# Up projection of a gated FFN by seven block products instead of eight, and its down-projection sums kept in DRAM

## The chip, the cores and the metric

One Trainium2 chip, one of its cores. The metric is the device time of one execution of the whole program in microseconds. The kernel before takes 2612.33 us (median of three runs, 2606.83 to 2616.81).

## The reference

One layer of a diffusion backbone on 512 tokens of 2048 features, all in float32. First a token mixer (a gated MLP with a spatial product), whose result is added to the stream. Then the part that the change touches:

```python
n_l = modulate(rmsnorm(h_lat, norm_g[i, 1]), m_l[:, :, 3], m_l[:, :, 4])
h_lat = h_lat + m_l[:, :, 5] * conv_ffn(n_l, ffn_w_up[i], ffn_conv_w[i], ffn_conv_b[i], ffn_w_down[i])
return rmsnorm(h_lat, final_g)

def conv_ffn(h, w_up, conv_w, conv_b, w_down):
    z = dwconv(h @ w_up, conv_w, conv_b, FFN_CONV // 2)   # width 3, over the tokens
    g, v = jnp.split(z, 2, axis=-1)
    return (jax.nn.silu(g) * v) @ w_down
```

`w_up` is 2048 x 11264 (a gate part `g` and a value part `v` of 5632 columns each), `w_down` is 5632 x 2048.

## The kernel before

Every tile has 128 partitions. Features lie on the partitions and the 512 tokens along the free axis, so a matmul takes a 128 x 128 block of weights as the stationary operand and a 128 x 512 tile of tokens as the moving one. A float32 operand is split into two float32r parts, high and low (`split`, lines 69 to 71: ScalarE copies the high part, VectorE subtracts it), and a product is three matmuls: high by high, high by low, low by high (`mm3`, line 64). Weights come in loads of 512 KB into a pool of six buffers, `r`; the split parts, `wh` and `wl`, have three buffers each. One such load with its matmuls is a *unit*. The weights of a unit are loaded and split two units ahead (`LOOK = 2`, line 878); with three buffers a split waits until TensorE has left the buffer of three units before.

The program is a list of units worked off by the loop at line 860. Other work (making normalised tiles, moving sums out of PSUM) is put in a list, `deferred`, and taken from it by `pop` at fixed places between the units. From this the framework's scheduler makes one instruction list for each engine; each engine works its own list off in order.

The FFN runs in eleven chunks of 512 columns of the gate part and the same columns of the value part. The normalised tokens are sixteen tiles `n2h`, `n2l`.

- **First chunk, gate part** (`f0_comp`, line 676): sixteen units, eight for each half of the tokens, since the norm's factors (`n_spread`) of the first half are known before those of the second. These matmuls have 256 columns, three times eight to a unit. Beside them `n_tile` (line 617) makes the normalised tiles.
- **First chunk, value part, and every later chunk** (`f_comp`, line 662): eight units for the gate part and eight for the value part, 24 matmuls of 512 columns each, into four PSUM banks.
- **Evacuation** (`conv_evac`, line 640): the width-3 convolution over the tokens, by ScalarE and VectorE straight out of PSUM; SiLU, the product with the gate, and a split into the operands of the down projection (`gated`).
- **Down projection** of the chunk before (`d_comp`, line 717): eight units, 24 matmuls of 512 columns each; VectorE adds each finished bank to the residual tile `ht[d]` in SBUF (`d_evac`, line 701).
- **Last chunk's down projection** (`e_comp`, line 787): in two halves of the tokens, with the final norm.

From the second chunk on the order is 16 units up, 8 units down.

Of the kernel before, what the change touches and what calls it, by code (L numbers as in the profile page):

```python
# [7 lines left out]
F32 = mybir.dt.float32  # L8
# [15 lines left out]
# the v half of w_in, as (column group, first K tile, end): short pieces while  # L24
# the modulation is still coming in
# [11 lines left out]
def build(tc, ctx, x, xT, cvec, adaT, ada_b, norm_g, w_in, g_v, w_sT, b_s, w_out,  # L37
# [6 lines left out]
    wpool = ctx.enter_context(tc.tile_pool(name="wpool", bufs=3))  # L44
# [14 lines left out]
    def mm(out, lhsT, rhs, first, last):  # L59
        nc.tensor.matmul(out, lhsT, rhs, start=first, stop=last)  # L60
# [3 lines left out]
    def mm3(out, sh, sl, mh, ml, first, last):  # L64
        mm(out, sh, mh, first, False)
        mm(out, sh, ml, False, False)
        mm(out, sl, mh, False, last)
# [22 lines left out]
    def load_cb():  # L90
        """silu(c) along every partition, by products that pick one row of [4, 512]."""
# [49 lines left out]
    def rstd_cols(ss, n, w, out=None):  # L141
        """1 / sqrt(ss / n + eps) of [P, w] sums: the table's root, then one Newton step."""
# [12 lines left out]
    def sum_cols(tiles, w):  # L155
        """Per-token sums over the feature partitions of the tiles: [P tokens, w] in PSUM."""
# [7 lines left out]
    def spread(r, w):  # L164
        """[P tokens, w] to [P, w * P], all tokens along every partition."""
# [138 lines left out]
    # the other tiles, in steps that are spread over the products  # L304
# [32 lines left out]

    deferred = []
# [6 lines left out]
    units = []          # (prep, comp, after)  # L345

# [100 lines left out]
    def sp_comp(cg, c4):  # L447
        # one moving operand holds both parts of the spatial weights side by side
# [60 lines left out]
    def sq_acc(key, d, ts=slice(0, T)):  # L509
        """Adds the square of a tile's tokens; the very last one is kept apart."""  # L510
# [51 lines left out]
    # the last K tiles of the second pass go in two halves of the tokens, so that  # L562
    # the norm of the first half runs under the products of the second
# [17 lines left out]
    def oh_comp(th, i):  # L581
        def f(w):
# [26 lines left out]
    n2h, n2l = [None] * ND, [None] * ND  # L609

    nstat, n2r = {}, {}
    made = [0, 0]

# [313 lines left out]
```

## Time and profile before

| | |
|---|---|
| median of three runs | 2612.33 us (2606.83 to 2616.81) |
| profiled execution, from its first instruction to its last | 2610.5 us |
| TensorE busy in it | 2560.6 us, 98% |
| VectorE busy | 1408.2 us, 54% |
| ScalarE busy | 855.5 us, 33% |
| GpSimd busy | 0.7 us |
| DMA, mean over the span | 138 GB/s |

What the device spends around the first and last instruction is not shown apart; the span lies 1.8 us under the median of the runs and inside their spread. Three stretches matter. The first chunk's gate part runs from 1149.6 to 1197.5 us, its value part to 1241.0, and then ten chunks of 130.6 us each follow, up to 2546.6. The rest, to 2610.5, is the last down projection with the final norm.

The engines' names in the rows are PE (TensorE matmul), PEld (TensorE weight load), DVE (VectorE), ACT (ScalarE), POOL (GpSimd) and SP (SyncE, which issues DMAs). In a row "wl<-r,wh" is the tile written and the tiles read; "b" is any tile of the general pool of 70, "p" a PSUM bank.

### The profile page before, as it was taken

The page shows a single profiled execution, that of the slowest core. Times are in us where ns is not written, and L with a number is a line of the kernel's source. Part 1 is how long each engine was busy: PE and PEld are TensorE (multiplying, and loading weights), DVE is VectorE, ACT ScalarE, POOL GpSimd, SP SyncE. Part 2 cuts the span into 40 slices and gives each one's busy share as a digit, 9 for nine tenths or more (in the row PEclk, how much of TensorE's full clock was granted, in tenths as well). Part 3 has the DMA queues.
Part 4 walks back from the last instruction along what each step waited for, and adds up shares of the span by engine and source line. Part 5 has one row for each costly group of instructions (what it writes and reads, how often), then busy time and mean ns, then how long its engine had stood idle before and what let it go on. Part 6 is the DMA issues. An engine that isn't in the chain of part 4 may idle for free.

```text
span 2610.5 us, 29733 instructions
## 1 busy us (share of the span) xinstructions
PE 2560.6 (98%) x11816; PEld 2135.1 (82%) x11816; DVE 1408.2 (54%) x2179; ACT 855.5 (33%) x1211; POOL 0.7 (0%) x6
## 2 busy tenths in 40 slices
PE   6999999999999999999999999999999999999998
PEld 5888788788888888898888888888888888888888
DVE  6885578666566446465453535353535353535365
ACT  7422234333334224355322222222222222222234
POOL 0000000000000000000000000000000000000000
PEclk9999999999999999999999999999999999999998
DMA  7886555555555446524233333333333333323331
GB/s 265 293 284 198 173 173 179 174 171 177 177 168 193 154 145 194 185 82 133 96 97 97 98 96 97 96 98 96 97 97 97 96 98 97 97 97 97 96 104 65
DMA packets 157556, 360.84 MB, mean 138 GB/s; under 512 B 12132, under 2 KB 18404, under 8 KB 157416
## 3 DMA queue, kind: packets, MB, share of 16 engines
q1 hardware_dynamic: 155304, 356.84, 42.1%
q10 hardware_dynamic: 2112, 2.10, 0.2%
q8 instruction: 92, 1.51, 0.2%
q14 instruction: 48, 0.39, 0.0%
HBM read 354.70 MB, written 4.19 MB: 137 GB/s over the span
## 4 chain that ended last, share of the span: by engine, by line
PE 76%; DMA 12%; DVE 8%; issue 3%; ACT 1%; SPq 0%; DVEq 0%; ACTq 0%
PE p L60 76%; DMA r<-in_adaT 10%; DVE wl L71 3%; DVE r L129 2%; DMA r<-in_w_in 1%; DVE b L361 1%; ACT wh L70 0%; DVE b L462 0%; DVE sp L444 0%; DVE b L465 0%; DVE b L71 0%; DVE r L781 0%; ACT b L268 0%; DVE b L356 0%; ACT b L70 0%
## 5 line engine op out<-in xcount | busy, mean ns | idle before, releaser
L60 PE MATMUL p<-b,wh 128*128 128x512 f32 (+1 forms) x6208 | 1883.5, 386 | 0.0
L60 PEld LDWEIGHTS p<-b,wh 128*128 128x128 f32 x6208 | 1158.0, 188 | 230.8
L60 PE MATMUL p<-b,wl 128*128 128x512 f32 (+1 forms) x3104 | 1196.0, 385 | 0.0
L71 DVE TENSOR_TENSOR wl<-r,wh 128x1024 fp32r<-128x1024 f32 (+1 forms) x457 | 550.9, 1206 | 795.7 <-ACT wh L70 793.5
L70 ACT ACTIVATE wh<-r 128x1024 fp32r<-128x1024 f32 (+1 forms) x457 | 478.2, 1047 | 1503.9 <-PE p L60 1474.9
L60 PEld LDWEIGHTS p<-b,wl 128*128 128x128 f32 x3104 | 584.5, 188 | 116.8
L129 DVE SCALAR_TENSOR_TENSOR r<-r,cb 128x1024 f32<-128x1024 f32 x192 | 233.6, 1223 | 295.5 <-DMA r<-in_adaT 295.1
L60 PE MATMUL p<-wh,b 128*128 128x512 f32 x992 | 314.1, 395 | 1.7 <-ACT wh L70 1.7
L60 PEld LDWEIGHTS p<-wh,b 128*128 128x128 f32 x992 | 188.4, 190 | 41.6 <-ACT wh L70 2.7
L60 PE MATMUL p<-wl,b 128*128 128x512 f32 x496 | 195.9, 395 | 8.8 <-DVE wl L71 8.8
L701 DVE SCALAR_TENSOR_TENSOR b<-p,m,b 128x512 f32<-128x512 f32 x160 | 118.0, 748 | 42.7 <-PE p L60 42.6
L60 PEld LDWEIGHTS p<-wl,b 128*128 128x128 f32 x496 | 94.4, 190 | 31.4 <-DVE wl L71 11.9
L60 PE MATMUL p<-b 128*128 128x256 f32 (+1 forms) x624 | 84.5, 296 | 5.3 <-ACT b L70 5.3
L60 PEld LDWEIGHTS p<-b 128*128 128x128 f32 x624 | 79.1, 193 | 9.0 <-ACT b L70 6.7
L70 ACT ACTIVATE b<-t 128x512 fp32r<-128x512 f32 (+1 forms) x91 | 48.8, 549 | 38.1 <-DVE t L654 37.5
L71 DVE TENSOR_TENSOR b<-t,b 128x512 fp32r<-128x512 f32 (+1 forms) x91 | 53.0, 592 | 10.6 <-ACT b L70 9.4
L60 PE MATMUL p<-sp 128*128 128x256 f32 x256 | 40.5, 294 | 9.2 <-DVE sp L444 8.3
L361 DVE TENSOR_TENSOR b<-p,b 128x512 f32<-128x512 f32 x76 | 48.9, 682 | 0.0
L60 PEld LDWEIGHTS p<-sp 128*128 128x128 f32 x256 | 36.2, 192 | 15.1 <-DVE sp L444 12.0
L71 DVE TENSOR_TENSOR b<-b 128x512 fp32r<-128x512 f32 (+2 forms) x69 | 43.3, 660 | 4.1 <-ACT b L70 4.0
L443 ACT ACTIVATE sp<-b,rv 128x128 fp32r<-128x128 f32 x128 | 42.1, 388 | 7.4 <-DVE sp L444 4.6
L645 ACT ACTIVATE t<-p,cw 128x512 f32<-128x512 f32 x44 | 34.2, 776 | 23.4 <-PE p L60 12.2
(86 smaller groups left out, 777.0 us busy)
## 6 DMA issues: line engine op xcount, KB each, us to landing
r<-in_adaT SPq DMA_DIRECT2D x192, 512.0 KB, 4.5
r<-in_w_up SPq DMA_DIRECT2D x184, 512.0 KB, 3.5
r<-in_w_in SPq DMA_DIRECT2D x121, 512.0 KB, 4.4
r<-in_w_down SPq DMA_DIRECT2D x88, 512.0 KB, 3.6
r<-in_w_out SPq DMA_DIRECT2D x64, 512.0 KB, 4.6
b<-in_x SPq DMA_DIRECT2D x16, 256.0 KB, 5.4
b<-in_xT SPq DMA_DIRECT2D x16, 256.0 KB, 5.2
r<-in_w_in SPq DMA_DIRECT2D x14, 256.0 KB, 4.1
```

The costliest lines, as they stand in the source:

```text
L60: nc.tensor.matmul(out, lhsT, rhs, start=first, stop=last)
L70: nc.scalar.activation(hi, src, AF.Copy)
L71: nc.vector.tensor_sub(lo, src, hi.bitcast(F32))
L129: nc.vector.scalar_tensor_tensor(r[b], r[b], 1.0, state["cb"][b], op0=ALU.mult, op1=ALU.mult, accum_out=m2[:, b, j:j + 1])
L361: nc.vector.tensor_add(b, p, b)
L443: nc.scalar.activation(vh[:, ns], v, AF.Copy, scale=rv[:, n:n + 1])
L645: nc.scalar.activation(t, p, AF.Identity, bias=cw[:, 3, ct:ct + 1], scale=cw[:, 1, ct:ct + 1])
L701: nc.vector.scalar_tensor_tensor(ht[d], p, m[:, 5 * ND + d:5 * ND + d + 1], ht[d], op0=ALU.mult, op1=ALU.add)
```

## The change

1. **Seven block products.** In the chunks after the first, the up projection treats two K tiles, two blocks of 128 weight columns and the two halves of the tokens as a 2 x 2 by 2 x 2 product of blocks and forms it by Strassen's method in Winograd's form: seven products in place of eight. A unit holds two pairs of K tiles, so 2 x 7 x 3 = 42 matmuls of 256 columns; a group of four units (`up_group`) gives two output tiles. `s_prep` forms four sums of weight blocks on VectorE (lines 778 to 780) before it splits seven blocks of 128 columns for each K pair; `s_evac` recombines the seven sums from four banks into the two output tiles, in SBUF (`z`), and `conv_evac` reads `z`.
2. **Sums of the tokens.** `n_tile` normalises in place and `t_pair` forms the sums of token blocks once, as new float32r tiles `x1` to `x4`. The first chunk keeps the eight plain products, by halves of the tokens (`f_mm`); its value part (`f1_comp`) goes by halves too, so it has 384 matmuls of 256 columns in place of 192 of 512.
3. **Residual in DRAM.** The new tiles take the room of `ht`. The residual is written to a DRAM tile `hD` at the end of the mixer (32 DMAs on SP's queue, in `oh_comp`). `d_evac` is now a ScalarE copy out of PSUM with the gate as scale, into a pool `part` of three buffers, and a DMA from GpSimd's queue that adds the tile to `hD`: 16 in each of ten chunks. Beside the last of them the sixteen tiles are read back.
4. **Order.** From the second chunk on: one group of four units, four units down, one group, four units down, two groups; in the last such round two, two and then four units down, these with the loads of the last chunk's weights.
5. **Small things.** The pool of split weights has four buffers, not three. `w_up` is laid out by blocks in DRAM. The signs of odd output tiles are put into the convolution's weights (two small VectorE instructions in `late_consts`). The pop after a unit comes behind the next load from the FFN on.

```diff
-    wpool = ctx.enter_context(tc.tile_pool(name="wpool", bufs=3))
+    wpool = ctx.enter_context(tc.tile_pool(name="wpool", bufs=4))
+    part = ctx.enter_context(tc.tile_pool(name="part", bufs=3))
+    dram = ctx.enter_context(tc.tile_pool(name="dram", bufs=1, space=bass.MemoryType.DRAM))
...
             sq_acc("2", 8 + i, ts)
+            for d in (i, 8 + i):
+                nc.sync.dma_start(out=hD[d * P:(d + 1) * P, ts], in_=ht[d][:, ts])
...
+    def t_pair(p):
+        def f():
+            e, o = ht[2 * p], ht[2 * p + 1]
+            t = tmp_t()
+            nc.vector.tensor_sub(t[:, L], o[:, R], e[:, R])
+            nc.vector.tensor_sub(e[:, R], e[:, L], e[:, R])
+            nc.vector.scalar_tensor_tensor(o[:, R], e[:, R], -1.0, o[:, R], op0=ALU.mult, op1=ALU.subtract)
+            nc.vector.scalar_tensor_tensor(t[:, R], o[:, R], -1.0, o[:, L], op0=ALU.mult, op1=ALU.subtract)
+            h, l = pair_t(x2, p)
+            split(h[:, R], l[:, R], e[:, R])
+            split(*pair_t(x3, p), t)
+            x4[p] = blk_t(F32R)
+            split(x4[p][:, L], x4[p][:, R], o[:, R])
+            tmade[0] += 1
         return f
...
+        if th == 1:
+            for p in range(NP):
+                deferred.append(t_pair(p))
...
+    def s_prep(cp, u):
+        def f():
+            r = wload(w_up[cp, u].rearrange("p k b -> p k b"), 2, 512).rearrange(
+                "p (k b c) -> p k b c", k=2, b=4)
+            s = raw.tile([P, 1024], F32, tag="r", name="s").rearrange("p (k b c) -> p k b c", k=2, b=4)
+            nc.vector.tensor_add(s[:, :, 0:2, :], r[:, :, 0:1, :].to_broadcast([P, 2, 2, P]), r[:, :, 1:4:2, :])
+            nc.vector.tensor_add(s[:, :, 2, :], s[:, :, 1, :], r[:, :, 1, :])
+            nc.vector.tensor_add(s[:, :, 3, :], s[:, :, 2, :], r[:, :, 2, :])
...
+            for src, b in ((r[:, :, 1:4, :], 3), (s, 4)):
...
+                split(*hl, src)
...
+    def s_evac(cp, acc):
...
+            nc.scalar.activation(at(3), d[:, L], AF.Copy)
+            nc.vector.tensor_add(two(z)[:, :, L], dup(at(3)), two(c))
+            nc.vector.tensor_add(two(at(5, 2)), dup(at(4)), two(a))
+            nc.vector.tensor_add(at(1, 2), at(5, 2), b)
+            nc.vector.tensor_add(at(3), at(6), a[:, L])
...
+                for out, (sh, sl), q, mov, new in (
+                        (d[:, L], (h3, l3), 0, lo(X1), True),
+                        (c[:, L], (h3, l3), 1, hi(X1), True),
+                        (c[:, R], (h4, l4), 2, X4, False),
+                        (a[:, L], (h4, l4), 1, hi(X2), True),
+                        (a[:, R], (h4, l4), 0, lo(X3), False),
+                        (b[:, L], (h4, l4), 3, lo(X2), True),
+                        (b[:, R], (h3, l3), 2, hi(X3), False)):
+                    mm3(out, sh[:, k, q, :], sl[:, k, q, :], *mov, first and new, last, True)
...
     def d_evac(fc, d, p):
         def f():
-            nc.vector.scalar_tensor_tensor(ht[d], p, m[:, 5 * ND + d:5 * ND + d + 1], ht[d],
-                                           op0=ALU.mult, op1=ALU.add)
+            t = part.tile([P, T], F32, tag="a", name="a")
+            nc.scalar.activation(t, p, AF.Copy, scale=m[:, 5 * ND + d:5 * ND + d + 1])
+            nc.gpsimd.dma_start(out=hD[d * P:(d + 1) * P, :], in_=t, accum_op=ALU.add)
+            if fc == NFC - 2:
+                ht[d] = blk_t()
+                nc.gpsimd.dma_start(out=ht[d], in_=hD[d * P:(d + 1) * P, :])
...
     for fc in range(1, NFC):
-        up_units(fc)
-        for q in range(8):
-            last = fc == NFC - 1
-            units.append((d_prep(fc - 1, q), d_comp(fc - 1, q), e_prep(q) if last else None))
+        last = fc == NFC - 1
+        up_group(fc, 0, 0)
+        down(fc - 1, range(0, 2 if last else 4))
+        up_group(fc, 0, 1)
+        if last:
+            down(fc - 1, range(2, 4))
+        else:
+            down(fc - 1, range(4, 8))
+        up_group(fc, 1, 0)
+        up_group(fc, 1, 1)
...
```

The instruction lists show where the work stands now. First place: VectorE, in the second half of the first chunk's gate part. "wl<-r,wh" is the split of a unit's weights, L626 (L652 after) the first step of a normalised tile, "b<-t,b" or "b<-b" with 256 columns the low part of one. Before:

```order
L71 TENSOR_TENSOR wl<-r,wh 128x1024
L150 SCALAR_TENSOR_TENSOR st<-st 128x2
L151 TENSOR_TENSOR st<-st 128x2
L71 TENSOR_TENSOR b<-t,b 128x256
L152 SCALAR_TENSOR_TENSOR st<-st 128x2
L71 TENSOR_TENSOR b<-t,b 128x256
L626 TENSOR_TENSOR t<-p,b 128x256 x2
L71 TENSOR_TENSOR wl<-r,wh 128x1024
L71 TENSOR_TENSOR b<-t,b 128x256 x2
```

After, from the last normalised tile of the second half on (L671 to L674 are the sums of `t_pair`, "b<-t,b" with 512 columns its largest split):

```order
L652 TENSOR_TENSOR b<-p,b 128x256 x2
L671 TENSOR_TENSOR t<-b 128x256
L73 TENSOR_TENSOR wl<-r,wh 128x1024
L672 TENSOR_TENSOR b<-b 128x256
L73 TENSOR_TENSOR b<-b 128x256 x2
L673 SCALAR_TENSOR_TENSOR b<-b 128x256
L73 TENSOR_TENSOR b<-b 128x256
L674 SCALAR_TENSOR_TENSOR t<-b 128x256
L671 TENSOR_TENSOR t<-b 128x256
L73 TENSOR_TENSOR wl<-r,wh 128x1024
L73 TENSOR_TENSOR b<-t,b 128x512
L672 TENSOR_TENSOR b<-b 128x256
```

The normalised tiles, two to a unit before, are now all ahead of the split for the eleventh of the sixteen units, and from there one `t_pair` stands between each unit's split and the next.

Second place: VectorE inside a chunk. Before, at the end of a value part (L646, L648 the convolution, L654 the product with the gate):

```order
L71 TENSOR_TENSOR wl<-r,wh 128x1024 x7
L646 SCALAR_TENSOR_TENSOR t<-p,cw,t 128x511
L648 SCALAR_TENSOR_TENSOR t<-p,cw,t 128x511
L646 SCALAR_TENSOR_TENSOR t<-p,cw,t 128x511
L654 TENSOR_TENSOR t<-t,b 128x512
L648 SCALAR_TENSOR_TENSOR t<-p,cw,t 128x511
L71 TENSOR_TENSOR b<-t,b 128x512
```

After, between two groups that follow each other with no unit of the down projection between them (L778 to L780 the sums of weights, L803 to L806 the recombination, L699 and L701 the convolution):

```order
L803 TENSOR_TENSOR z<-z,p 128x2x256
L804 TENSOR_TENSOR z<-z,p 128x512
L778 TENSOR_TENSOR s<-r 128x2x256
L73 TENSOR_TENSOR wl<-r,wh 128x768
L73 TENSOR_TENSOR wl<-s,wh 128x1024
L805 TENSOR_TENSOR z<-z,p 128x512
L806 TENSOR_TENSOR z<-z,p 128x256
L779 TENSOR_TENSOR s<-s,r 128x2x128
L780 TENSOR_TENSOR s<-s,r 128x2x128
L699 SCALAR_TENSOR_TENSOR b<-z,cw,b 128x511 x2
L73 TENSOR_TENSOR wl<-r,wh 128x768
L73 TENSOR_TENSOR wl<-s,wh 128x1024
```

One unit's split has become five VectorE instructions, and the recombination of the group before stands among them.

Third place: ScalarE at the end of four units of the down projection. Before (L645 the convolution's first step, "b<-t" a high part of `gated`):

```order
L70 ACTIVATE wh<-r 128x1024 x7
L645 ACTIVATE t<-p,cw 128x512 x2
L70 ACTIVATE b<-t 128x512
L70 ACTIVATE wh<-r 128x1024
L645 ACTIVATE t<-p,cw 128x512
```

After (L847 the copy of a finished bank; "128x768" and "128x1024" the two high parts of the first and second unit of the next group):

```order
L72 ACTIVATE wh<-r 128x768
L704 ACTIVATE b<-b 128x512
L847 ACTIVATE a<-p,m 128x512 x3
L72 ACTIVATE wh<-s 128x1024
L847 ACTIVATE a<-p,m 128x512
L72 ACTIVATE wh<-r 128x768
L847 ACTIVATE a<-p,m 128x512 x3
L72 ACTIVATE wh<-s 128x1024
L847 ACTIVATE a<-p,m 128x512
```

Eight copies stand between the high parts of the next two units, and each from the fourth on also waits for the adding DMA of the copy three before it, which has to give its buffer back.

## Rows read from the trace of the kernel before

**Rows 1.** First part of the page: busy time, share of the span, instructions.
```profile
PE 2560.6 (98%) x11816; PEld 2135.1 (82%) x11816; DVE 1408.2 (54%) x2179; ACT 855.5 (33%) x1211; POOL 0.7 (0%) x6
```

**Rows 2.** Windows by stage; last columns: granted clock, DMA share, GB/s.
```profile
core 0: us, PE busy (x) PEld busy (x) DVE busy (x) ACT busy (x) POOL busy (x), PEclk, DMA share, GB/s
...
1149.60:1197.50 47.90, 47.90 (x398) 47.57 (x397) 40.20 (x80) 41.36 (x78) 0.00 (x0) 1.00 0.49 155
1197.50:1241.00 43.50, 43.50 (x194) 36.03 (x193) 17.47 (x21) 14.54 (x18) 0.00 (x0) 1.00 0.34 109
1241.00:1371.60 130.60, 130.60 (x577) 108.12 (x577) 63.32 (x75) 39.34 (x47) 0.00 (x0) 1.00 0.30 97
1371.60:1502.20 130.60, 130.60 (x578) 108.13 (x577) 56.70 (x64) 35.92 (x41) 0.00 (x0) 1.00 0.30 97
2416.00:2546.60 130.60, 130.60 (x578) 108.15 (x577) 63.57 (x78) 42.09 (x54) 0.00 (x0) 1.00 0.30 97
```

**Rows 3.** Timeline, TensorE, 256 columns: start us, length us, instruction.
```profile
1149.60 0.40 PE L60 MATMUL p<-b,wh 128*128 128x256 f32 x2
1149.84 0.28 PE L60 MATMUL p<-b,wl 128*128 128x256 f32 x1
1149.96 0.40 PE L60 MATMUL p<-b,wh 128*128 128x256 f32 x2
```

**Rows 4.** Timeline, TensorE, inside a later chunk, 512 columns.
```profile
1333.53 0.62 PE L60 MATMUL p<-b,wh 128*128 128x512 f32 x2
1333.99 0.39 PE L60 MATMUL p<-b,wl 128*128 128x512 f32 x1
1334.21 0.62 PE L60 MATMUL p<-b,wh 128*128 128x512 f32 x2
```

**Rows 5.** Groups by line and shape: busy us, mean ns | idle before, releaser.
```profile
L71 DVE TENSOR_TENSOR wl<-r,wh 128x1024 fp32r<-128x1024 f32 x443 | 541.4, 1222 | 794.2 <-ACT wh L70 792.1
L70 ACT ACTIVATE wh<-r 128x1024 fp32r<-128x1024 f32 x443 | 469.6, 1060 | 1490.0 <-PE p L60 1461.3 <-DMA r<-in_w_in 21.6 <-issue 6.2
...
L701 DVE SCALAR_TENSOR_TENSOR b<-p,m,b 128x512 f32<-128x512 f32 x160 | 118.0, 748 | 42.7 <-PE p L60 42.6
...
L71 DVE TENSOR_TENSOR b<-t,b 128x512 fp32r<-128x512 f32 x59 | 40.5, 686 | 9.9 <-ACT b L70 9.4
...
L70 ACT ACTIVATE b<-t 128x512 fp32r<-128x512 f32 x59 | 37.0, 627 | 38.0 <-DVE t L654 37.5
...
L645 ACT ACTIVATE t<-p,cw 128x512 f32<-128x512 f32 x44 | 34.2, 776 | 23.4 <-PE p L60 12.2 <-DVE b L71 11.2
...
L646 DVE SCALAR_TENSOR_TENSOR t<-p,cw,t 128x511 f32<-128x511 f32 x44 | 32.7, 744 | 0.9
...
L750 DVE SCALAR_TENSOR_TENSOR b<-p,m,b 128x256 f32<-128x256 f32 x32 | 15.4, 483 | 10.7 <-PE p L60 9.9
...
L626 DVE TENSOR_TENSOR t<-p,b 128x256 f32<-128x256 f32 x32 | 12.4, 416 | 0.3
```

**Rows 6.** Waits: engine, line, waited for; us in total, times, longest.
```profile
ACT wh L70 <- PE p L60: 1474.9, 396, 5.8
```

**Rows 7.** Timeline, VectorE, second half of the first chunk's gate part.
```profile
1178.52 1.23 DVE L71 TENSOR_TENSOR wl<-r,wh 128x1024 fp32r<-128x1024 f32 x1 [0.16 <-ACT wh L70]
1179.81 0.76 DVE L71 TENSOR_TENSOR b<-t,b 128x256 fp32r<-128x256 f32 x2
1180.49 0.75 DVE L626 TENSOR_TENSOR t<-p,b 128x256 f32<-128x256 f32 x2
1181.40 1.23 DVE L71 TENSOR_TENSOR wl<-r,wh 128x1024 fp32r<-128x1024 f32 x1 [0.16 <-ACT wh L70]
```

**Rows 8.** DMA issues: KB each, median us from issue to landing.
```profile
r<-in_w_up SPq DMA_DIRECT2D x184, 512.0 KB, 3.5
...
b<-in_x SPq DMA_DIRECT2D x16, 256.0 KB, 5.4
...
out_T<-r SPq DMA_DIRECT2D x4, 256.0 KB, 3.1
```

More of the change, by code (lines that the diff above doesn't have):

```diff
@@ L57, in bank, with mm, mm3 @@
         return ps.tile([P, 512], F32, tag="p", name="p")
[L59 to L67, printed above, removed]
+    def mm(out, lhsT, rhs, first, last, shared=False):
+        nc.tensor.matmul(out, lhsT, rhs, start=first, stop=last, skip_group_check=shared)
+    def mm3(out, sh, sl, mh, ml, first, last, shared=False):
+        mm(out, sh, mh, first, False, shared)
+        mm(out, sh, ml, False, False, shared)
+        mm(out, sl, mh, False, last, shared)
     def split(hi, lo, src):
@@ L606, in build @@
             units.append((lambda: None, oh_comp(th, i), None))
-    n2h, n2l = [None] * ND, [None] * ND
+    F0 = len(units)
+    NP = ND // 2
+    x1, x2, x3, x4, b12 = [{} for _ in range(5)]
+    hD = dram.tile([D, T], F32, name="hD")
     nstat, n2r = {}, {}
     made = [0, 0]
+    tmade = [0]
     def n_sum(th):
@@ L693, in f @@
             pop(2)
-            if th == 1 and k2 == ND // 2 - 1:
+            if th == 1 and k2 == NP - 1:
                 for i in range(4):
@@ new lines, in s_comp, with f @@
+    def s_comp(fc, i2, vpart, u):
+        cp = vpart * (FF // 256) + fc * 2 + i2
+        def f(w):
+            (h3, l3), (h4, l4) = w
+            while tmade[0] < min(2 * u + 2, NP):
+                pop()
+            if u == 0:
+                state["sp7"] = [bank() for _ in range(4)]
+            a, b, c, d = state["sp7"]
+            for k in range(2):
+                p = 2 * u + k
+                X1, X2, X3 = x1[p], x2[p], x3[p]
+                X4 = x4[p][:, L], x4[p][:, R]
+                lo = lambda x: [y[:, L] for y in x]
+                hi = lambda x: [y[:, R] for y in x]
+                first, last = p == 0, p == NP - 1
+                for out, (sh, sl), q, mov, new in (
[7 more added lines that the diff above has]
+                    mm3(out, sh[:, k, q, :], sl[:, k, q, :], *mov, first and new, last, True)
+            if u == NP // 2 - 1:
+                deferred.append(s_evac(cp, state["sp7"]))
+                for i in range(2):
+                    deferred.append(lambda i=i: conv_evac(
+                        fc, 2 * i2 + i, vpart, state["z", cp][:, i * T:(i + 1) * T])())
+        return f
@@ L807, in e_comp, with up_group, down, twice @@
         return f
-    def up_units(fc):
-        for vpart in range(2):
-            c0 = vpart * FF + fc * 512
-            src = lambda k2, c0=c0: w_up[k2 * 256:(k2 + 1) * 256, c0:c0 + 512]
-            if fc == 0 and vpart == 0:
-                for th in range(2):
-                    for k2 in range(ND // 2):
-                        units.append((half_prep(src, k2), f0_comp(th, k2), None))
-                continue
-            for k2 in range(ND // 2):
-                units.append((half_prep(src, k2), f_comp(fc, vpart, k2), None))
-    up_units(0)
-    for fc in range(1, NFC):
-        up_units(fc)
-        for q in range(8):
-            last = fc == NFC - 1
-            units.append((d_prep(fc - 1, q), d_comp(fc - 1, q), e_prep(q) if last else None))
+    for th in range(2):
+        for k2 in range(NP):
+            units.append((f_prep(0, k2), f0_comp(th, k2), None))
+    for k2 in range(NP):
+        units.append((f_prep(1, k2), f1_comp(k2), None))
+    def up_group(fc, i2, vpart):
+        cp = vpart * (FF // 256) + fc * 2 + i2
+        for u in range(NP // 2):
+            units.append((s_prep(cp, u), s_comp(fc, i2, vpart, u), None))
+    def down(fc, qs, after=None):
+        for q in qs:
+            units.append((d_prep(fc, q), d_comp(fc, q), after and after(q)))
+    for fc in range(1, NFC):
+        last = fc == NFC - 1
[4 more added lines that the diff above has]
+            down(fc - 1, range(2, 4))
+        else:
+            down(fc - 1, range(4, 8))
+        up_group(fc, 1, 0)
+        up_group(fc, 1, 1)
+        if last:
+            def twice(q):
+                a, b = e_prep(2 * (q - 4)), e_prep(2 * (q - 4) + 1)
+                return lambda: (a(), b())
+            down(fc - 1, range(4, 8), twice)
     for th in range(2):
@@ L867, in build @@
         comp(ready.pop(i))
-        pop(1)
+        if i < F0:
+            pop(1)
         if after:
```

118 lines of the change are left out of this document (85 added, 33 removed).

## The prediction

> **What bounds the kernel now.** The first part of the page says that TensorE is busy for 2560.6 of 2610.5 us, VectorE for 1408.2 and ScalarE for 855.5 [rows 1]. [...] The list of waits agrees: its longest entry is ScalarE's split waiting for TensorE to give a weight buffer back, 1474.9 us [rows 6]. So in the FFN time is the number of matmuls times what one costs, as long as splits and evacuation keep up.
>
> What one costs is read from starts, not lengths, since matmuls overlap. In a later chunk three matmuls of 512 columns start every 0.68 us (1333.53 to 1334.21), 226.7 ns each [rows 4]. With 256 columns three start every 0.36 us, 120 ns each [rows 3]. Halving the columns thus does not halve the price: twice 120 is 13 ns more than 226.7. A matmul count of seven eighths in equal columns is therefore worth less than an eighth.
>
> **The change, part by part.**
>
> *Up projection, ten chunks.* Before: 16 units x 24 = 384 matmuls x 226.7 ns = 87.0 us. After: 16 units x 42 = 672 x 120 ns = 80.6 us. That is 6.4 us a chunk, 64 us in ten. The new matmuls have the shape of [rows 3], with the stationary operand in the same pattern (high, high, low).
>
> *First chunk, value part.* 384 x 120 ns = 46.1 us in place of 43.5 [rows 2]: +2.6 us.
>
> *First chunk, gate part.* Here cover is thin, and t_pair comes in. One unit lasts 24 x 120 ns = 2.88 us on TensorE; VectorE's work for it (one split, two normalised tiles) runs from 1178.52 to 1181.24, and with 0.16 us of waiting that is 2.88 as well [rows 7]. A t_pair has two sums and two small splits like L626 (0.42 us each), two instructions like L750 (0.48), and a 512-column split (0.69) [rows 5]: 3.3 us, some 2.9 when they overlap by the 0.08 us that [rows 7] show (0.76 for two, not 0.84). By the new order all normalised tiles of the second half stand ahead of the eleventh unit's split. The second half's factors come after four units, at about 1162 us; then sixteen tiles (0.715 us each by [rows 7]) and six splits (1.2) keep VectorE until about 1181, where TensorE would want the eleventh unit at 1179.3. From there each unit needs a split and one t_pair, 4.0 to 4.5 us, against 2.88: 1.4 us late, six times over until the value part begins, whose units are long enough. With the 1.7 us at its start that is 10 us. Bounds: nothing, if the buffers' lead of up to four units covers it; 26 us, if all eight t_pairs lie open (8 x 3.3). I take 10.
>
> *Splits and sums of weights.* A unit had one split: 1.22 us on VectorE, 1.06 on ScalarE. Now VectorE does a 512-column sum (0.69), two of 256 (0.42 each), and splits of 768 (0.95, between the 512 and 1024 of [rows 5]) and 1024 (1.22): 3.70 us; ScalarE copies 768 and 1024, 1.9 us. A group's recombination is four VectorE instructions, 2.5 us. For a whole chunk VectorE had about 61 us (mean of three windows of [rows 2]); it loses 16 x 1.22 and, by d_evac, 16 x 0.75, and gains 16 x 3.70 and 4 x 2.5: 99 of 124 us. ScalarE goes from 39 to 67 with 16 copies at about 0.78 (L645). Averages fit; the place to look is where three groups follow one another (two at the end of a chunk's list, one at the next one's start). There TensorE needs 12 x 5.04 = 60.5 us, some 61.3 with the preparation that falls in the last two down units, and VectorE 12 x 3.70 + 2 x 2.5 + one gate evacuation (4 x 0.744 = 3.0) + one value evacuation (3.0 + 4 x 0.69 = 5.7) + 1.6 of waiting for ScalarE inside the latter = 59.7 us, or 55 when overlapped. Walked through in order, each low part is ready 4 to 4.8 us after its buffer comes free, and is wanted after 5.04 plus about 1.3 us, since the first eleven matmuls of a unit do without the last of them. [Rows 7] show VectorE and ScalarE handing on at 94% without a gap on TensorE. So this is nearly covered. Bounds: 0, and 2.2 us a chunk if nothing overlaps and each of the 24 splits waits 0.16. I take 0.8, 8 us in all.
>
> *Accumulating DMAs.* No GpSimd DMA is in the trace. ScalarE's fourth copy waits for the first DMA, the seventh for the fourth, and behind the seventh stands the high part for the second unit of the next group. With the copies at the pace of TensorE (1.36 us a bank) and L from the end of a copy to its DMA's landing, that unit's last low part is ready 6.0 + 2L us after the second down unit starts; it is wanted 3 x 5.44 + 5.04 + 1.3 = 22.7 us after. So L up to 8.3 us costs nothing, and each us beyond it costs 2 us twice a chunk, 40 us in all. Bounds from the nearest rows of 256 KB: a write lands in 3.1 us, a load in 5.4; one after the other, at double length, would be 10.8 [rows 8]. I take a little over the load's, 5.5: no cost. At 10.8 it costs 100 us. [...]
>
> *The rest.* The 32 writes of the residual sit in SP's queue among loads that run up to six buffers ahead; those at the end of the mixer come behind nine loads of w_up. The sixteen read-backs land during the last 64 us; the last round's extra splits (16 x 0.63 on ScalarE, 16 x 0.69 on VectorE) lie beside four down units, 21.8 us. One us for all this. The fourth weight buffer may win a little in the mixer; bound -4 us, taken as 0.
>
> *Sum.* Against the profiled span: 2610.5 - 64 + 2.6 + 10 + 8 + 1 = 2568 us; the median lies 1.8 us above that span, so **2570 us**, 1.6% faster.
>
> **Rivals.**
> - *Slow accumulation* (slower). Place: ScalarE's copies; price 40 us for each us of L over 8.3; it decides from 9.4, where it eats the gain of 42. At 10.8 the time is 2670. For it: reading and writing the same DRAM bytes, and a queue nothing has used. Against: it needs nearly twice the slowest 256 KB row, at a DMA share of 0.30.
> - *VectorE becomes the bound* in the runs of three. The sums read blocks in strides and one block twice over, which no row shows. If all its instructions there cost 5% more than their rows, and nothing overlaps, they need 62.7 + 24 x 0.16 = 66.5 us against 61.3: 5.2 us a chunk in place of 0.8, 2614 us. Against: lengths in [rows 5] follow the element count alone, in PSUM and SBUF.
> - *All hidden.* The buffers' lead covers the t_pairs and the group boundaries: 2612 - 64 + 2.6 = 2551 us.
> [...]
> - *No cheaper product.* Alternating between half banks makes a 256-column matmul cost 130 ns (87.0 us / 672), and nothing is won: 2630 with the costs above. The same shape at 120 in [rows 3] speaks against it.
>
> **How the numbers follow.** Forecast 0.60 (its own range 2555 to 2588), slow accumulation 0.10, VectorE-bound 0.12, all hidden 0.12, port lock 0.03, no cheaper product 0.03. A change of 0.5%, 13 us, is about what can be told from none. Faster: the forecast, all hidden and a third of VectorE-bound, 0.76; the same: half of VectorE-bound and a fifth of slow accumulation, 0.08 with 0.02 of the others, 0.10; slower 0.14. Below 2547 I leave 0.04, above 2606 about 0.16.
>
> **What would show it.** In the windows: a chunk of 124 to 125.5 us, TensorE without gaps, VectorE near 90 to 99 us of it; the first chunk's gate part at 55 to 60 us with TensorE waiting for "wl" some 1 to 2 us a unit from the eleventh on. The ScalarE copies of d_evac waiting for DMA by over a us each would say that L is near its limit. The forecast is wrong if a chunk is over 127 us, if the waits for VectorE lie mainly inside the chunks, or if the 256-column matmuls inside a group start more than 125 ns apart.

## The result, and the profile after

The changed kernel takes 2536.07 us (median of four runs, 2533.04 to 2538.2) against 2610.15 beside it: a ratio of 0.9707, 95% interval 0.969 to 0.9724. That is 74 us won where 42 were forecast, and the time lies below the range. Medians here and below are of fast executions; one of the kernel before that took 7711.14 us is left out. The profiled execution is 79.2 us shorter than that of before (2531.3 against 2610.5). The first part of its page:

```profile
PE 2488.6 (98%) x14888; PEld 2223.9 (88%) x14888; DVE 1759.8 (70%) x2877; ACT 1100.1 (43%) x1595; POOL 149.4 (6%) x182
```

Against [rows 1], TensorE issues a quarter more matmuls and is busy 72 us less; VectorE has 352 us more to do. Cut by stage (windows; two that split the first chunk, three of the ten chunks, and the last part):

```profile
core 0: us, PE busy (x) PEld busy (x) DVE busy (x) ACT busy (x) POOL busy (x), PEclk, DMA share, GB/s
1128.10:1174.20 46.10, 45.44 (x376) 44.83 (x375) 43.87 (x102) 40.50 (x83) 0.00 (x0) 1.00 0.40 123
1174.20:1223.50 49.30, 46.93 (x389) 46.52 (x389) 34.75 (x59) 20.24 (x30) 0.00 (x0) 1.00 0.28 86
1226.70:1350.90 124.20, 124.20 (x866) 116.67 (x865) 90.42 (x129) 60.83 (x79) 14.01 (x16) 1.00 0.54 132
1350.90:1475.00 124.10, 124.10 (x866) 116.58 (x865) 89.92 (x129) 59.66 (x77) 13.91 (x16) 1.00 0.56 136
...
2344.10:2468.30 124.20, 124.20 (x863) 116.43 (x863) 97.23 (x140) 63.96 (x89) 16.88 (x23) 1.00 0.60 168
2468.30:2531.30 63.00, 51.17 (x425) 50.71 (x423) 37.54 (x102) 30.61 (x67) 6.41 (x9) 0.92 0.38 106
```

The FFN's first matmul starts at 1128.1 us, not 1149.6, and the last part at 2468.3. Ten chunks of 124.16 us (16 units x 42 x 120 ns and 8 x 5.44) end there, so by this sum they begin at 1226.7, and TensorE has no gap in them. With [rows 2] this gives the account:

| stretch | before | after | change | forecast |
|---|---|---|---|---|
| ahead of the FFN | 1149.6 | 1128.1 | -21.5 | 0 (bound -4) |
| first chunk, both parts | 91.4 | 98.6 | +7.2 | +12.6 (2.6 and 10) |
| ten chunks | 1305.6 | 1241.6 | -64.0 | -56 (-64 and 8) |
| last part | 63.9 | 63.0 | -0.9 | +1 |
| span | 2610.5 | 2531.3 | -79.2 | -42.4 |

The largest miss is in a part that the forecast hardly looked at. The same 550 us there, windows of before and after:

```profile
240.00:790.00 550.00, 534.07 (x2410) 441.90 (x2409) 359.72 (x699) 180.55 (x308) 0.00 (x0) 0.98 0.55 174
```

```profile
240.00:790.00 550.00, 542.95 (x2496) 452.03 (x2495) 382.61 (x732) 193.72 (x330) 0.00 (x0) 1.00 0.56 180
```

Before, TensorE stood still for 15.9 us and ran at a granted clock of 0.98; after, 7.1 us at 1.00. One such gap of before, in VectorE's timeline (in brackets the idle time ahead and what ended it):

```profile
516.59 1.23 DVE L129 SCALAR_TENSOR_TENSOR r<-r,cb 128x1024 f32<-128x1024 f32 x1 [3.24 <-DMA r<-in_adaT]
...
517.74 0.48 DVE L462 SCALAR_TENSOR_TENSOR b<-p,gv,bst 128x256 f32<-128x256 f32 x1
518.14 1.22 DVE L71 TENSOR_TENSOR wl<-r,wh 128x1024 fp32r<-128x1024 f32 x1
...
520.06 0.34 DVE L444 SCALAR_TENSOR_TENSOR sp<-b,rv,sp 128x128 fp32r<-128x128 f32 x1
```

and TensorE's beside it:

```profile
518.52 0.28 PE L60 MATMUL p<-sp 128*128 128x256 f32 x1
520.46 0.50 PE L60 MATMUL p<-sp 128*128 128x256 f32 x2 [1.66 <-DVE sp L444]
...
521.86 0.95 PE L60 MATMUL p<-b,wh 128*128 128x512 f32 x2
522.60 0.63 PE L60 MATMUL p<-b,wl 128*128 128x512 f32 x1
523.03 1.05 PE L60 MATMUL p<-b,wh 128*128 128x512 f32 x2
```

VectorE stood 3.24 us for a row of the modulation ("r<-in_adaT"). Then it had the row's product (L129), a split and three small instructions (L462 twice, L465) ahead of the spatial tile "sp" that TensorE wanted at 518.8. After the gap three matmuls take 1.17 us from start to start (521.86 to 523.03) in place of the 0.68 of [rows 4]. The granted clock of the window behind the gap is 0.59:

```profile
521.80:526.00 4.20, 4.20 (x14) 3.29 (x14) 1.86 (x4) 1.19 (x4) 0.00 (x0) 0.59 0.19 72
```

At 0.59 these 4.2 us did the work of 2.5 (4.2 x 0.59), by estimate: about 1.7 us lost on top of the gap's 1.66.

### The profile page after: what moved, and what is told of

The parts are those of the page before. It is cut to its first block, busy times and chain, and to the rows that moved or that the text cites. A ratio compares the mean times of both kernels' runs of the same rounds, so it can differ in the third digit from the quotient of the medians.

```text
span 2531.3 us, 37809 instructions
## 1 busy us (share of the span) xinstructions
PE 2488.6 (98%) x14888; PEld 2223.9 (88%) x14888; DVE 1759.8 (70%) x2877; ACT 1100.1 (43%) x1595; POOL 149.4 (6%) x182
## 4 chain that ended last, share of the span: by engine, by line
PE 83%; DMA 7%; DVE 7%; issue 2%; ACT 1%; SPq 0%; DVEq 0%; ACTq 0%
PE p L62 83%; DMA r<-in_adaT 6%; DVE r L131 2%; DVE wl L73 2%; DMA r<-in_w_in 1%; ACT wh L72 1%; DVE b L367 0%; DVE b L73 0%; DVE b L468 0%; DVE sp L450 0%; DVE b L471 0%; DVE b L362 0%; DVE r L930 0%; ACT b L270 0%; ACT b L72 0%
## 5 line engine op out<-in xcount | busy, mean ns | idle before, releaser
L62 PE MATMUL p<-b,wh 128*128 128x256 f32 (+1 forms) x8256 | 1905.4, 325 | 0.1
L62 PEld LDWEIGHTS p<-b,wh 128*128 128x128 f32 x8256 | 1388.9, 190 | 126.2 <-ACT wh L72 0.3
L62 PE MATMUL p<-b,wl 128*128 128x256 f32 (+1 forms) x4128 | 1340.0, 325 | 2.9 <-DVE wl L73 2.8
L72 ACT ACTIVATE wh<-r 128x1024 fp32r<-128x1024 f32 (+2 forms) x457 | 438.2, 969 | 970.2 <-PE p L62 792.3
L62 PEld LDWEIGHTS p<-b,wl 128*128 128x128 f32 x4128 | 784.6, 190 | 68.0 <-DVE wl L73 3.7
L73 DVE TENSOR_TENSOR wl<-r,wh 128x1024 fp32r<-128x1024 f32 (+2 forms) x457 | 505.0, 1110 | 207.7 <-ACT wh L72 207.0
L848 POOL DMA_DIRECT2D hD<-a x160 | 139.7, 907 | 2294.8 <-ACT a L847 2293.8
L73 DVE TENSOR_TENSOR wl<-s,wh 128x1024 fp32r<-128x1024 f32 x160 | 195.6, 1222 | 106.6 <-ACT wh L72 106.6
L62 PEld LDWEIGHTS p<-wh,b 128*128 128x128 f32 x992 | 186.2, 188 | 40.0 <-ACT wh L72 1.9
L778 DVE TENSOR_TENSOR s<-r 128x512 f32<-128x512 f32 x160 | 110.0, 688 | 100.5 <-DMA r<-in_w_up 99.5
L72 ACT ACTIVATE wh<-s 128x1024 fp32r<-128x1024 f32 x160 | 167.6, 1048 | 19.5 <-PE p L62 19.4
L847 ACT ACTIVATE a<-p,m 128x512 f32<-128x512 f32 x160 | 109.0, 686 | 127.6 <-DMA hD<-a 79.8
L780 DVE TENSOR_TENSOR s<-s,r 128x256 f32<-128x256 f32 x160 | 67.7, 423 | 3.8
L779 DVE TENSOR_TENSOR s<-s,r 128x256 f32<-128x256 f32 x160 | 67.6, 422 | 3.8
```

What stands on the lines that cost most here:

```text
L62: nc.tensor.matmul(out, lhsT, rhs, start=first, stop=last, skip_group_check=shared)
L72: nc.scalar.activation(hi, src, AF.Copy)
L73: nc.vector.tensor_sub(lo, src, hi.bitcast(F32))
L778: nc.vector.tensor_add(s[:, :, 0:2, :], r[:, :, 0:1, :].to_broadcast([P, 2, 2, P]), r[:, :, 1:4:2, :])
L779: nc.vector.tensor_add(s[:, :, 2, :], s[:, :, 1, :], r[:, :, 1, :])
L780: nc.vector.tensor_add(s[:, :, 3, :], s[:, :, 2, :], r[:, :, 2, :])
```

## The experiments

### Who won the 21.5 us

**e1_before_w4.** The kernel before with the fourth buffer alone.

```diff
-    wpool = ctx.enter_context(tc.tile_pool(name="wpool", bufs=3))
+    wpool = ctx.enter_context(tc.tile_pool(name="wpool", bufs=4))
-    nc = bacc.Bacc("TRN2", target_bir_lowering=False, num_devices=1)
+    nc = bacc.Bacc("TRN2", target_bir_lowering=False, num_devices=1, dynamic_dma_scratch_size=2048)
```

> The kernel before with four weight buffers in place of three and nothing else of the change (the room comes from a smaller scratch for GpSimd DMAs, which it does not use). Theory: the 21.5 us that the part ahead of the FFN won come from the fourth buffer, so this kernel takes 2610 - 21 = about 2589 us, its FFN still starts 130.6 us chunks, and the granted clock of the stretch 240 to 787 us is 1.00 instead of 0.98. Rival: they come from another edit (the residual's writes, the order of the instructions) or from chance: 2610 us.

2593.79 us against 2610.31, ratio 0.9937 (0.9922 to 0.9953): 16.5 us; in the traces the FFN starts 17.4 us earlier. Gaps between 240 and 790 us fell from 15.7 to 6.4 by the waits, and the clock rose to 1.00.

**e6_before_scratch.** The second line of that edit alone.

> The kernel before with only the smaller scratch for GpSimd DMAs that the first experiment also had, and three weight buffers. Theory (the buffer did it): 2611 us. Rival (the scratch did it): 2594 us.

2609.35 against 2612.41, ratio 0.9991 (0.9979 to 1.0004): the scratch has no effect that these runs can show.

**e2_after_m3.** After every third split ahead of the FFN, a spare tile is taken from the weight pool and left alone.

> The changed kernel with the weight buffers used three at a time ahead of the FFN (after every third split the fourth buffer is passed over) and four in the FFN. Theory: 2536 + 21 = 2557 us, the FFN starts at about 1149 us instead of 1128, gaps of TensorE before splits and spatial tiles come back between 240 and 790 us, with a granted clock below 1.00 there. Rival, another edit did it: 2536 us, FFN at 1128.

2534.31 us. This experiment failed in its making: the spare tile, which nothing reads or writes, held no buffer back (between 240 and 787 us TensorE is busy for 539.7 us, in the changed kernel for 540.0), so what ran was in effect the changed kernel once more. It serves as a second time of it.

**e5_after_hold.** The same aim, with a tile that is used.

```diff
+    kept = [wpool.tile([P, 1024], F32R, tag=t, name="kept") for t in "hl"]
+    for t in kept:
+        nc.vector.memset(t[:, 0:2].bitcast(F32), 0.0)
...
+            if th == 1 and i == 0:
+                for t in kept:
+                    u = small.tile([P, 2], F32, tag="u", name="u")
+                    nc.vector.tensor_add(u, t[:, 0:2].bitcast(F32), ht[8][:, 0:2])
```

> The changed kernel with one of its four weight buffers held by a tile that two tiny VectorE instructions write at the start and read just ahead of the FFN, so that only three go round until there. Theory (the fourth buffer won the 21.5 us): 2536 + 21 = 2557 us, the first FFN matmul at about 1149 us instead of 1128, granted clock below 1.00 between 240 and 790 us. Rival (another edit did it): 2536, FFN at 1128.

2553.11 us, 17 to 19 above the changed kernel's two times (2536.07, 2534.31); the gaps are 17.3 us again. So the fourth weight buffer is worth some 17 us in both kernels. The other 4 of the 21.5 belong to no edit that was tried alone; the runs of one kernel differ by as much.

### How a weight buffer does that

**e11_before_sp, e9_best.** The first idea was ScalarE's queue: a split that waits for TensorE holds up what stands behind it, there 297.4 us in the 550 of before. Both kernels write the spatial tiles ahead of a unit's matmuls in the program (e9 on top of e3 below).

```diff
                 sp_comp(cg, k2 - 3)
+            if 2 <= k2 < 6:
+                sp_prep(cg, k2 - 2)
...
-            after = (lambda cg=cg, k2=k2: sp_prep(cg, k2 - 2)) if 2 <= k2 < 6 else None
-            units.append((half_prep(src, k2), u_comp(cg, k2), after))
+            units.append((half_prep(src, k2), u_comp(cg, k2), None))
```

> The kernel before, three weight buffers, with sp_prep ahead of a unit's matmuls in place of behind them, nothing else. Theory: a weight split that waits for its buffer holds up what stands behind it on ScalarE, here the spatial tiles; so the 8.9 us of gaps before spatial matmuls and the low clock behind them (0.98 over 372 us, some 7 us) go without a fourth buffer: 2595 to 2602 us. Rival (the buffers' lead itself is what counts): 2610.

> The changed kernel with the t_pairs in the value part (as in the experiment on them, 2528.7 us) and the spatial tiles' copies and splits (sp_prep) written ahead of a unit's matmuls, not behind them, so that ScalarE does not meet the next weight split, which waits for TensorE, first. Theory (what stands behind a waiting split is late with it): the three gaps of 5.8 us before spatial matmuls go, and about 2 us of lower clock behind one of them: about 2522 us. Rival (VectorE's share of these tiles is what is late, not ScalarE's place in the queue): 2529.

2611.96 against 2613.55 (ratio 0.9992, 0.9983 to 1.0002) and 2530.1 against e3's 2528.67: nothing. But these two failed in their making as well. The framework's scheduler makes each engine's list, and the traces of e11 and before, and those of e9 and e3, show the same instructions in the same order on VectorE, ScalarE, GpSimd and SP's queue. The copy of a spatial tile still stands behind the split, before:

```profile
518.49 1.06 ACT L70 ACTIVATE wh<-r 128x1024 fp32r<-128x1024 f32 x1 [4.19 <-PE p L60]
520.50 0.40 ACT L443 ACTIVATE sp<-b,rv 128x128 fp32r<-128x128 f32 x1 [0.95 <-DVE sp L444]
```

and in e11:

```profile
520.99 1.06 ACT L70 ACTIVATE wh<-r 128x1024 fp32r<-128x1024 f32 x1 [4.19 <-PE p L60]
523.32 0.40 ACT L443 ACTIVATE sp<-b,rv 128x128 fp32r<-128x128 f32 x1 [1.27 <-DVE sp L444]
```

So the idea was not tested. What speaks against it in this gap is that ScalarE's copy at 520.50 came after a wait for VectorE. The traces also had VectorE's wait for modulation rows in common. In these 550 us of before, and of after:

```profile
DVE r L129 <- DMA r<-in_adaT: 190.9, 70, 5.7
```

```profile
DVE r L131 <- DMA r<-in_adaT: 156.7, 63, 4.7
```

With three weight buffers it is 181.0 to 190.9 us in four traces (before, e5, e6, e11), with four and the other pools of before 156.0 to 162.3 in ten (after, e1 to e4, e7 to e10, e16). Kernels below with other pools lie between (165.5 to 173.6 in e13, e14 and e15) or, with five weight buffers and fewer blocks (e12), at 186.2.

**e13_before_raw8.** The kernel before, three weight buffers, eight load buffers: `raw` from 6 to 8, with the scratch of e6.

> The kernel before with eight load buffers in place of six, three weight buffers, and the smaller scratch that makes room. Theory (the chain is load buffer, modulation load, VectorE: a load waits until a split or a dot product gives its buffer back, VectorE stands still until the modulation row has landed, 190.9 us between 240 and 790, and splits and spatial tiles stand behind it; a fourth weight buffer only lets the splits give load buffers back sooner): more load buffers do the same, VectorE's waits for these rows fall below 160 us, 2590 to 2597 us. Rival (the weight buffers' own lead counts): 2610 us.

2597.93 against 2612.49, ratio 0.9948 (0.9932 to 0.9965): 14.6 us without a fourth weight buffer, and 0.9 us above the theory's range. The wait, which was to fall below 160 us, is 168.5, and the gaps are 12.1 us, so the chain that the theory named came out only in part. Part of the gain is won in the first 100 us, where TensorE is busy 82.5 us, not 79.2.

**e16_late_dot.** On e3: a row's dot products one unit behind its load.

```diff
+    rode = []
...
     def ride(i):
+        while rode:
+            j, r = rode.pop(0)
+            ada_dot(j, 0, r)
+            ada_dot(j, 1, r)
...
-                    r = ada_load(j)
-                    ada_dot(j, 0, r)
-                    ada_dot(j, 1, r)
...
+                    rode.append((j, ada_load(j)))
```

> The changed kernel with t_pairs in the value part and the dot products with a modulation row put one unit behind its load in VectorE's order, so that VectorE does not stand still for the row. Theory (what stands behind the waiting dot product is late with it): the 158 us of VectorE's waits for the rows mostly go, the 6 us of gaps too: 2521 to 2526 us. Rival (the rows then hold two load buffers a unit longer, and the weights' loads come later): 2529 or more.

2528.88 us, and VectorE waits 162.3 us, which is the rival's time. But the scheduler gave SP's queue the list of e3, and VectorE the list of e3 but for a few small instructions and splits at two places; a row's product stands where it stood. In e3:

```profile
500.11 1.22 DVE L73 TENSOR_TENSOR wl<-r,wh 128x1024 fp32r<-128x1024 f32 x1
506.17 1.23 DVE L131 SCALAR_TENSOR_TENSOR r<-r,cb 128x1024 f32<-128x1024 f32 x1 [4.83 <-DMA r<-in_adaT]
```

and in e16:

```profile
500.31 1.22 DVE L73 TENSOR_TENSOR wl<-r,wh 128x1024 fp32r<-128x1024 f32 x1
506.03 1.23 DVE L131 SCALAR_TENSOR_TENSOR r<-r,cb 128x1024 f32<-128x1024 f32 x1 [4.50 <-DMA r<-in_adaT]
```

So this run is e3 once more, and whether a later product would help stays open.

**e17_before_norows.** The kernel before without these loads.

```diff
-                    r = ada_load(j)
-                    ada_dot(j, 0, r)
-                    ada_dot(j, 1, r)
+                    for b in range(2):
+                        r = raw.tile([P, 1024], F32, tag="r", name="r")
+                        nc.vector.scalar_tensor_tensor(r, state["cb"][b], 1.0, state["cb"][b], ...)
```

> The kernel before, three weight buffers, without the 96 loads of modulation rows (2 x 512 KB each... of 48 rows) that ride beside the units; their dot products are made from the resident vector instead, into the same load buffers, so VectorE has the same instructions and never waits for a row (three parts of the modulation are thus wrong). Theory (VectorE's waits for these rows, 190.9 us between 240 and 790, put splits and spatial tiles behind them late): the gaps of TensorE there (15.7 us) mostly go without a fourth weight buffer: 2588 to 2597 us. Rival (the gaps come from the weight buffers' lead, whatever VectorE waits for): 2610.

(It is 128 loads, 64 rows and four parts of the modulation; the expectation miscounted.) 2580.31 us against 2610.09, ratio 0.9886 (0.9869 to 0.9903): 30 us, more than the theory's 13 to 22. The window and VectorE's waits in it:

```profile
240.00:790.00 550.00, 550.00 (x2546) 460.08 (x2545) 386.35 (x730) 195.14 (x332) 0.00 (x0) 1.00 0.32 96
```

```profile
DVE wl L71 <- ACT wh L70: 92.4, 47, 5.2
DVE b L462 <- PE p L60: 48.1, 27, 3.8
```

With three weight buffers, six load buffers and all of VectorE's instructions, not one gap is left and the clock is 1.00. So the gaps do not arise without the loads of modulation rows. The gap above shows how: VectorE stands still until a row is in, and what is queued behind it comes late to TensorE (3.24 us for the row, then a gap of 1.66 us ahead of the spatial tile). The run also takes away the traffic (96 GB/s against 174) and the time that a row in flight holds a load buffer, so it does not part the wait for a row from what its transfer does to the weights' loads; in this window of before no compute engine's wait is put down to a load of weights, though.

How a fourth weight buffer shortens the waits was not shown. That it gives load buffers back a unit sooner agrees with the time of e13. A rival stands beside it: with other pools the scheduler also makes other lists. Behind the spatial tile at 521 us of before, VectorE goes straight to a row:

```profile
520.71 0.87 DVE L444 SCALAR_TENSOR_TENSOR sp<-b,rv,sp 128x128 fp32r<-128x128 f32 x3
524.14 1.23 DVE L129 SCALAR_TENSOR_TENSOR r<-r,cb 128x1024 f32<-128x1024 f32 x1 [2.56 <-DMA r<-in_adaT]
```

In e1 a split stands between the two, and the row is in by then:

```profile
512.21 1.13 DVE L444 SCALAR_TENSOR_TENSOR sp<-b,rv,sp 128x128 fp32r<-128x128 f32 x4
513.25 1.22 DVE L71 TENSOR_TENSOR wl<-r,wh 128x1024 fp32r<-128x1024 f32 x1
514.50 1.23 DVE L129 SCALAR_TENSOR_TENSOR r<-r,cb 128x1024 f32<-128x1024 f32 x1
```

In e13 a split follows the spatial tile there, too (at 511.35 us). No run keeps the order and changes a pool alone, so the buffers and the order are not parted.

### The terms inside the FFN

**e3_tpair_f1.** The `t_pair`s go into the value part, one to a unit.

```diff
-        if th == 1:
-            for p in range(NP):
-                deferred.append(t_pair(p))
...
                 for i in range(4):
+                    deferred.append(t_pair(i))
                     deferred.append(conv_evac(0, i, 0, state["fp"][i]))
+                for p in range(4, NP):
+                    deferred.append(t_pair(p))
...
```

> The changed kernel with the eight t_pairs moved out of the first chunk's gate part into its value part, one to a unit. Theory: first chunk's two parts take 98.6 us in the changed kernel against 94.0 for their matmuls (47.9 as before and 384 x 120 ns); the 4.6 us are t_pairs ahead of splits, so they go: 2531 us, no TensorE gap between 1128 and 1225. Rival: VectorE is full there as well (8 x 3.1 + 8 x 1.22 + 4 x 1.5 = 40.6 of 46.1 us), the gaps move into the value part: 2536 us or a little more.

2528.67 us (ratio to before 0.969, 0.9674 to 0.9705), 5.6 below e2's 2534.31, which ran on the same chip. TensorE's waits for splits in the first chunk, in the changed kernel:

```profile
1165.53 0.39 PE L62 MATMUL p<-b,wl 128*128 128x256 f32 x1 [0.43 <-DVE wl L73]
1177.25 0.39 PE L62 MATMUL p<-b,wl 128*128 128x256 f32 x1 [1.14 <-DVE wl L73]
1180.66 0.39 PE L62 MATMUL p<-b,wl 128*128 128x256 f32 x1 [1.24 <-DVE wl L73]
```

They are gone in e3, where 1128 to 1227 us show TensorE busy throughout:

```profile
1128.00:1227.00 99.00, 99.00 (x828) 99.00 (x828) 84.43 (x169) 65.14 (x119) 0.00 (x0) 1.00 0.35 110
```

(Its trace has five short gaps before splits in the last round instead, 1.8 us in all, so the margin there is thin.)

**e7_dve1, e8_dve2.** The first sum of weight blocks is made twice, and three times.

```diff
             nc.vector.tensor_add(s[:, :, 0:2, :], r[:, :, 0:1, :].to_broadcast([P, 2, 2, P]), r[:, :, 1:4:2, :])
+            nc.vector.tensor_add(s[:, :, 0:2, :], r[:, :, 0:1, :].to_broadcast([P, 2, 2, P]), r[:, :, 1:4:2, :])
```

> The changed kernel with the first sum of weight blocks made twice: one more VectorE instruction of 512 columns in each of the 160 units. In a run of three groups VectorE is busy 50.4 of 60.4 us; twelve more instructions at 0.61 to 0.69 make 57.7 to 58.7. Theory (only VectorE's total in the run counts, and it has 10 us to spare): 2536 us, no TensorE gap in the chunks. Rival (each unit's split is on a chain of its own, without slack, as the 0.8 us a chunk of the prediction had it): at least 12 x 0.6 = 7 us a chunk, 2606 us.

> The changed kernel with the first sum of weight blocks made three times: two more VectorE instructions of 512 columns in each of the 160 units. Theory: 50.4 + 24 x 0.61 to 0.69 = 65 to 67 us of VectorE in a run of three groups that lasts 60.4, so TensorE waits 4.6 to 6.6 us a chunk: 2582 to 2602 us, more if the clock falls behind the gaps. Rival (VectorE is no bound here, the splits run far enough ahead): 2536.

2535.02 and 2567.24 us. One more instruction of 0.69 us in each of 160 units costs nothing that the median shows; of two, 31 us show. No gap was expected in e7's chunks; its trace has seven in the last three of them, 4.0 us in all. The changed kernel's run of three groups, and the waits of TensorE in e8's chunks:

```profile
1310.60:1371.00 60.40, 60.40 (x503) 60.27 (x502) 50.43 (x72) 28.05 (x37) 0.97 (x2) 1.00 0.44 127
```

```profile
PE p L62 <- ACT wh L72: 19.0, 17, 1.5
PE p L62 <- DVE wl L73: 2.8, 10, 0.3
```

TensorE waits mostly for ScalarE's high part here, but ScalarE was itself held up by VectorE's last sum of weights ("s"), as ahead of a wait of 1.47 us at 1366.9:

```profile
1365.54 0.38 ACT L804 ACTIVATE z<-p 128x256 f32<-128x256 f32 x1 [4.72 <-DVE s L782]
1365.82 1.05 ACT L72 ACTIVATE wh<-s 128x1024 fp32r<-128x1024 f32 x1
```

VectorE has 10 us to spare in a run of three groups of the changed kernel, enough for twelve instructions and not for 24. That the limit is reached between them agrees with the theory; its range began at 46 us, so it was too high by a third or more.

**e4_part2.** Two buffers, not three, for the tiles that are added to the residual.

> The changed kernel with two buffers for the copies that are added to the residual, not three. Each copy from the third on waits for the adding DMA two before it, so the seventh comes after three of them one after the other: 3 x (5.2 + 0.69) + 0.69 = 18.4 us, and the split behind it some 3.5 us later, against 22.7 us until it is wanted. Theory (the adding DMAs' time is hidden by a margin, which this uses up): 2536 to 2566 us, about 0.7 us twice a chunk, 2550. Rival (these waits are not on any path to TensorE): 2536 us.

2595.61 us, 60 above the changed kernel and twice the most that was expected. Waits in its trace:

```profile
ACT a L847 <- DMA hD<-a: 221.5, 76, 5.3
...
PE p L62 <- ACT wh L72: 22.6, 16, 3.0
PE p L62 <- DVE wl L73: 20.9, 28, 2.6
```

The margin is real and two buffers overrun it: the copies wait 221.5 us for DMAs (79.8 with three), and TensorE, in all, 43.5 us for splits, which stand behind them (6.7 with three). The granted clock is 0.991 over the whole run, not 0.997, by estimate some 15 us more (0.006 of 2592.7). What is left of the 60 is not told apart.

**e10_plain.** `accum_op=ALU.add` left out.

> The changed kernel with plain writes in place of the accumulating DMAs; the residual in DRAM is thus overwritten, not added to. Same time expected, since the adding DMAs are hidden: 2536 us. What is asked is their landing time: 5.2 us with the adding; if reading the old values is most of it, 3 us without, and ScalarE's 79.8 us of waits for these DMAs go; if it is GpSimd's issue and the transfer alone, about 5.

2533.46 us in its one run. Landing of these DMAs, median, in the changed kernel and here:

```profile
hD<-a POOLq DMA_DIRECT2D x160, 256.0 KB, 5.2
```

```profile
hD<-a POOLq DMA_DIRECT2D x160, 256.0 KB, 3.4
```

Adding costs 1.8 us a tile, and the time shows none of it; ScalarE's waits fall from 79.8 to 27.1 us.

### Looking for a faster version

**e12_best_w5, e15_blk66, e14_raw7.** More buffers of one kind, paid for with blocks of the general pool: e9 with five weight buffers and 66 blocks, e3 with 66 blocks, e3 with seven load buffers and 68 blocks.

> The version with late t_pairs and early sp_prep, with five weight buffers and 66 blocks in place of 70. Theory (only gaps of TensorE are to be won, and ahead of the FFN behind the first 100 us some 1 to 3 us before splits are left): 2519 to 2522 us, no difference to the same with four that can be measured. Rival: four blocks fewer hold back normalised tiles or products and cost something: 2525 or more.

> The changed kernel with t_pairs in the value part and 66 blocks in place of 70, four weight buffers. With five weight buffers and 66 blocks the time was 16 us above this kernel's. If the missing blocks did that: about 2545 us. If the fifth buffer did it: 2529.

> The changed kernel with t_pairs in the value part, seven load buffers in place of six and 68 blocks in place of 70. Theory of the load buffers: VectorE's 158 us of waits for modulation rows fall further, and most of the 6 us of gaps between 240 and 790 us go: 2521 to 2526 us. Rivals: no more to win there, 2529; or the two blocks are missed: over 2532.

2546.37, 2535.2 and 2534.87 us: all slower than e3. Four blocks fewer cost some 6 us by e15; the other 10 of e12 are not explained. In e14 VectorE's wait is 173.6 us and the gaps are 11.0, where the theory of the load buffers said that both would fall; with 68 blocks it is no clean test, but it does not speak for the theory. The fastest version stays e3, 2528.67 us; e9 and e16 are in effect the same program.

## Why the prediction was wrong

**Ahead of the FFN, the step that failed.** "The fourth weight buffer may win a little in the mixer; bound -4 us, taken as 0." It won 17 us (e1, e5). The bound came from no row. The windows of [rows 2] start at 1149.6 us; one over 240 to 790 would have shown 15.9 us of gaps at a granted clock of 0.98, and the waits VectorE's 190.9 us for modulation rows. [Rows 6] give one sum over the span, which does not show the places where a split or a spatial tile came late. Of the 36.8 us by which the sum fell short of the profiled gain, this stretch holds 21.5, the group boundaries 8.0, the first chunk 5.4 and the rest 1.9. So the costs inside the FFN were too high as well: e5, with the buffer taken away, still took 2553.11 us, below the range's lower end of 2555.

**Ten chunks.** The main term, 64 us from 384 x 226.7 against 672 x 120 ns, is exact: [rows 3, 4] carry over, and TensorE has no gap in the chunks' windows before ([rows 2]) or after, so time there is the number of matmuls times what one costs. The 8 us at the group boundaries were zero. VectorE is busy 90 us of a chunk, where 99 were added up from [rows 5], and 50.4 in a run of three, where 55 to 59.7 were. Most of that is overlap: in one chunk (1350.9 to 1475.0 us) the lengths of its instructions add up to 96.3 us and cover 90.1. The sums in strides cost what was taken, 0.69 and 0.42 us, though lengths do not follow the element count alone, as one rival had it: at 512 columns [rows 5] have 686 and 748 ns. By e7 and e8 the slack ends between one and two more instructions a unit.

**First chunk.** The 2.6 us for halves hold; t_pair cost 4.6, not 10. The kind was right (gaps before splits, gone in e3), and the place nearly: the first gap comes at the thirteenth unit, not the eleventh, and the last lies in the value part. Three splits were late, not six, and by 0.4 to 1.2 us. That the buffers' lead took up the rest is likely but not shown. All four sums of a t_pair take 0.42 us, where two were taken at 0.48.

**Accumulating DMAs.** 5.5 us estimated, 5.2 measured, and hidden as said. The near hit is in part luck: the row taken was a load's, while by e10 it is a write of 3.4 us and 1.8 for adding. e4 shows the rival's mechanism (ScalarE's copies wait 221.5 us for these DMAs, 79.8 with three buffers) and that it was one buffer away.

**Rivals.** "Port lock" (0.03), GpSimd's issues holding VectorE up, is a term that no run shows; in the changed kernel the 160 issues do VectorE no harm that shows: the 28 first sums of weights (L778) that overlap an issue last 684 ns on average, the 132 others 688. The 256-column matmuls start 120 ns apart in half banks too (three from 1231.15 to 1231.51 us). "All hidden" came nearest, 2551 us, and less the 17 it is 2534; but the t_pairs were not hidden (4.6 us).

## What to carry to other kernels

A change has parts that work outside the stage it is meant for. For each, look at that stage's own windows for gaps and a clock below 1, and bound the part by them, not by a guess. A long wait of a helper engine is slack only if nothing behind it in its queue is wanted (here 3.24 us of VectorE, and 1.66 us of TensorE behind them). Where lengths in a profile overlap (96.3 us of them cover 90.1 here), add busy time from a window, not means from groups; and find a margin by adding work until it shows. Before an experiment that moves work is believed, its engines' lists have to be compared with those of the kernel it started from: three here changed the program's text and not the order that ran.

## What the runs showed of the hardware

In the kernel before, a TensorE gap of 1.66 us was followed by 4.2 us at a granted clock of 0.59, by the estimate above 1.7 us lost on top of it; other gaps of the same size, such as one of 2.05 us in the changed kernel (window 450 to 475 us, granted clock 1.00), were not. A DMA of 256 KB that adds to DRAM lands in 5.2 us (changed kernel, median of 160) against 3.4 for a plain write from the same queue (e10).
